# Two-layer encoder trunk on one core: sums of the modulation vectors moved to VectorE in the first phase, and to other places later on

## The chip, the core and the metric

The kernel runs on one core of a Trainium2 chip. The metric is the device time of one execution in microseconds (us), median over the runs. The engines of the core are TensorE (PE in the views, with PEld for its weight loads), VectorE (DVE), ScalarE (ACT), GpSimd (POOL) and SyncE (SP), which here only issues transfers. Each engine works through its own instructions in the order in which they were laid down. A scheduler of the framework lays that order down when the kernel is built, so it is not simply the order of the program text.

## The reference

For 256 tokens of width 2048 the trunk computes two layers and a final norm. Layer 0 is RWKV-7 time mixing and a squared-ReLU MLP of width 8192; layer 1 is attention in chunks of 64 tokens over a shared key and value, and another MLP. Each sub-layer is normed and modulated by vectors that come from the condition c (one vector of 2048):

```
for layer in range(DEPTH):
    mod = c @ w_ada[layer] + b_ada[layer]
    sh1, sc1, gt1, sh2, sc2, gt2 = jnp.split(mod, 6, axis=-1)
    if layer == N_A_LAYERS:
        sh_kv, sc_kv = jnp.split(c @ w_ada_kv + b_ada_kv, 2, axis=-1)
        ...
    h = modulate(rms_norm(x, g_mix[layer]), sh1, sc1)
    ...
    x = x + gt1[:, None, :] * y
    h = modulate(rms_norm(x, g_mlp[layer]), sh2, sc2)
    x = x + gt2[:, None, :] * sq_relu_mlp(h, w_up[layer], w_down[layer])
return rms_norm(x, g_final)
```

So there are 14 modulation vectors of 2048 numbers, each a product of c with a 2048 x 2048 matrix in float32 (16 MB to be read for each). This case is about where in the program, and on which engine, those products are formed.

## The kernel before

**Large products.** Every matrix product is split for precision. A tile of weights `raw` (128 x 1024, 512 KB) is loaded by SP, ScalarE casts it into `wH` (L367), and VectorE subtracts to get the rest `wL` (L370). PE then multiplies: a 512-column product with `wH` (L401) and a 256-column product with `wL` (L402) per tile of 128 inputs (`proj2`), or three products of 258 columns (L390 to L392, `proj`). There are three buffers each of `wH` and `wL`, and six of `raw`. SP issues all weight loads in one queue, in order, and an issue that waits for a free buffer holds those behind it.

**The first two modulation vectors** (scale and shift of layer 0, `ada_blocks`) are needed before anything else. They are made in eight blocks of 256 outputs. A block loads two parts of four tiles `rawa` (512 KB each, four buffers). Each tile holds four input tiles of 128 x 256. PE multiplies the four with a column of c repeated 32 times (`crep`) and puts them into four groups of 32 columns of the array (L666), so that the four run beside each other. ScalarE copies the sums to `adat` (L672), PE folds the four groups (L677), and VectorE adds the bias (`mod`, L683) and forms the gain (L685). The first block stands at the start of the program; the others are spread among the value projection, the LoRA products (`l`, from `mix` tiles that VectorE makes, L707) and the second half of that projection (`t`, added into `v` on VectorE, L734). This is phase 1; it ends near 217 us.

**The other twelve vectors** are summed up on VectorE. A step (`ada_step`) takes one tile of 128 x 1024 of a modulation matrix (`raw`, or `rada` where a pool of its own was opened by `ada_room`) and adds its product with one number of c per partition to `acc` (L441 for the first tile of 16, L443 for the others). There are 384 steps. After 16 of them PE folds `acc` (`ada_sum`, L465). The steps are spread over the program as follows:

- In the time mixing there are 19 periods of 16 slots. Six slots of each period take a step, from the third period (p = 2) on: 102 steps.
- In the first `out_proj` (the product with `w_o`, tiles n = 0 to 15), a pool of five `rada` buffers is open, tiles 8 and 9 take a step, and the last six tiles drain the queue.
- In the MLPs, `ada_tick` takes three steps in two tiles. Where a vector is needed and not complete, `ada_need` takes the missing steps at once; behind the up products of the first 16 tiles it asks for vector (0, 5), which is complete at step 128.
- At the end of the first MLP the last seven tiles drain the queue.

**Norms.** The sum of squares `ss` of the new x is complete when the last tile of `out_proj` or of an MLP is (VectorE adds the last part, L507). PE then sums it over the partitions (L512, in `rstd`), and VectorE and ScalarE make the factor `rstd` (`rv` L514, L519 to L521). To keep PE fed meanwhile, the next stage starts with eight output tiles on inputs that are not normed yet (the constant `RAW`), and multiplies by `rstd` afterwards (`late_norm`, L553 and L554). The product for `rstd` stands behind the first eight of the 16 input tiles of the first of them (constant `HK`).

In the period loop the slots that take a step are set by hand:

```
if slot in self.ADA_SLOTS and p >= 2:
    self.ada()
```

Of the kernel before, what the change touches and what calls it, by code (L numbers as in the profile page):

```python
# [12 lines left out]
F32 = mybir.dt.float32  # L13
# [304 lines left out]
class Body:  # L318
# [243 lines left out]
    def run(self):  # L562
# [22 lines left out]
        with ExitStack() as st:  # L585
# [6 lines left out]
            self.ada_need((0, 2), (0, 4), (0, 3))  # L592
            with self.ada_room(5):
                nxt = self.out_proj(self.pp, "w_o", self.y_hl, (0, 2), "g_mlp0", (0, 4), (0, 3), self.o_ps)
            sp.close()
# [24 lines left out]
    def layer_a(self, st, sp):  # L620
# [6 lines left out]
        with ExitStack() as s1:  # L627
# [22 lines left out]
            def ada_blocks():  # L650

                lo = 0
                for w_ in blocks:
                    W, ks = w_ * P, 8 // w_
                    ps = self.psm().rearrange("p (i n) -> p i n", i=2)
                    for part in (1, 0):
                        w, _ = self.ada_src(0, part)
                        w = w[:, lo * P:lo * P + W].rearrange("(a i p) n -> a p i n", p=P, i=ks)
                        for a in range(KT // ks):
                            raw = pb.tile([P, HK * P], F32, tag="rawa", bufs=4, name="rawa")  # L660
                            raw = raw.rearrange("p (i n) -> p i n", i=ks)
                            nc.sync.dma_start(out=raw, in_=w[a])
                            for i in range(ks):
                                kt = ks * a + i
                                g = 32 * (kt % 4)
                                nc.tensor.matmul(ps[g:g + 32, part, :W], crep[:, kt, :], raw[:, i, :],  # L666
                                                 start=(part == 1 and kt < 4), stop=(part == 0 and kt >= KT - 4),
                                                 tile_position=(0, g))
                            if part or a < KT // ks - 1:
                                yield  # L670
# [119 lines left out]
        with ExitStack() as s1:  # L790
# [50 lines left out]
            for p in range(NPAIR + 3):  # L841
# [11 lines left out]
                for slot in range(16):  # L853
# [9 lines left out]
                    self.fin(2)  # L863
                    if slot in self.ADA_SLOTS and p >= 2:
                        self.ada()
# [4 lines left out]
    def out_proj(self, pp, wname, hl, gate, g, sc, sh, begun=()):  # L870
# [5 lines left out]
        for n0 in range(0, KT, 2):  # L876
# [14 lines left out]
            for n, ps in zip((n0, n0 + 1), sums):  # L891
# [7 lines left out]
                self.ss_add(x, n, nc.vector if n == KT - 1 else None)  # L899
                if n < KT - 6 and (n >= 8 or not begun):  # L900
                    self.ada()
                elif n >= KT - 6:
                    self.ada_drain(1)
# [7 lines left out]
    def mlp(self, st, pp, layer, scaled, gain, shift, g=None, sc=None, sh=None):  # L911
# [8 lines left out]
        def up(q, f):  # L920
# [5 lines left out]
            if q == 0 and f < RAW:  # L926
                ins = self.proj(ps[:, :TE], w, lambda kt: scaled[:, kt], (0, HK))
                if rstd is None:
                    with tc.issue_after(ins):
                        rstd = self.rstd()  # L930
                self.proj(ps[:, :TE], w, lambda kt: scaled[:, kt], (HK, KT))
                self.late_norm(t, ps, rstd, ALU.max, 0.0)
            else:
                ps = ps.rearrange("p (i t) -> p i t", i=2)
                self.proj2(ps, w, lambda kt: hl[:, kt, :, 0:T])
                self.sum2(t, ps)
                nc.scalar.activation(t, t, AF.Relu)  # L937
# [7 lines left out]
        for q in range(NQ):  # L945
# [13 lines left out]
            for n in range(KT):  # L959
# [7 lines left out]
                if q == NQ - 1:  # L967
# [5 lines left out]
                    if g is None:  # L973
                        nc.scalar.activation(x, x, AF.Copy, scale=self.vec("g_final", n))
                if q == NQ - 1 and n >= KT - 7:
                    self.ada_drain(1)
# [9 lines left out]
    def attention(self, st, pp, scaled, kv_gain, kv_shift):  # L986
# [20 lines left out]
        for j in range(RAW):  # L1007
            ps = pp.tile([P, 512], F32, tag="pj", bufs=2, name="pj")
            w = self.weight(d["w_k_shared"][j])
            ins = self.proj(ps[:, :TE], w, lambda kt: scaled[:, kt], (0, HK))  # L1010
            if rstd is None:
                with tc.issue_after(ins):
                    rstd = self.rstd()
            self.proj(ps[:, :TE], w, lambda kt: scaled[:, kt], (HK, KT))
            self.late_norm(ks[:, j, :], ps, rstd, ALU.bypass, None)
# [158 lines left out]
```

## Time and profile before

| what | value |
|---|---|
| median of three runs | 2722.8 us (2720.47 to 2723.33) |
| the profiled execution | 2719.8 us, of which the span of the records is 2718.0 us |
| mean granted TensorE clock | 0.994 |
| DVE, ACT, POOL busy | 2072.1 us (76%), 1348.1 us (50%), 227.4 us (8%) |
| moved by DMA | 662.65 MB, 244 GB/s in the mean |

The stages in the trace of before are: phase 1 to about 217 us, the time mixing and its drain to about 750 us (the first row of L894 starts at 750.6), the first `out_proj` from there to 817 us (`rv` at 817.5), the first MLP to 1556 us, the attention with its two projections after that, and the second MLP to the end.

A row of the timeline gives the start, the duration, the engine, the line, what it writes and reads, and in brackets how long the engine was idle before it and what ended that. A row of the waits gives the engine, line and releaser, then the us in total, the number of times and the longest. A row of the windows gives the busy time of each engine in a stretch, then the mean granted TensorE clock (PEclk), the DMA share and the GB/s.

### The profile page before, as it was taken

The numbers are of one execution on the slowest core, as the hardware profiler recorded it, in microseconds if no ns is written. First come the engines' busy times: TensorE is split into PE (matmuls) and PEld (weight loads), VectorE is DVE, ScalarE is ACT, GpSimd is POOL, SyncE is SP. The second block draws the span as 40 slices with busy tenths as digits, with TensorE's granted clock in tenths as the row PEclk, the third lists the DMA queues.
The fourth block names the chain that finished last, engine by engine and source line by source line (L and its number), as shares of the span: only waits on it lengthen the run. The fifth ranks groups of instructions, "written<-read, shape, count | busy, mean of one in ns | idle before, by whom it ended". The sixth has DMA issues, their size and how long they took to land.

```text
span 2718.0 us, 58600 instructions
## 1 busy us (share of the span) xinstructions
PE 2649.5 (97%) x23786; PEld 2237.3 (82%) x23786; DVE 2072.1 (76%) x3045; ACT 1348.1 (50%) x2432; POOL 227.4 (8%) x368
## 2 busy tenths in 40 slices
PE   6999999999999999999999999999999999999997
PEld 3678777777889888888888898877898888888886
DVE  4568878877798988888888996898988555555555
ACT  2346544545356445445355454465565364453554
POOL 0002223323110000000000100000100000000002
PEclk9999999999999999999999999999999999999999
DMA  9876556554687988888888877887857555555553
GB/s 312 277 276 204 181 164 200 186 180 153 194 292 250 354 313 314 326 300 318 320 325 324 280 265 237 315 295 230 290 184 266 190 189 186 186 187 187 188 190 125
DMA packets 217390, 662.65 MB, mean 244 GB/s; under 512 B 21408, under 2 KB 68896, under 8 KB 217120
## 3 DMA queue, kind: packets, MB, share of 16 engines
q1 hardware_dynamic: 215056, 656.36, 70.4%
q8 instruction: 187, 3.06, 0.5%
q10 hardware_dynamic: 2064, 2.54, 0.3%
q14 instruction: 83, 0.68, 0.1%
HBM read 656.72 MB, written 2.10 MB: 242 GB/s over the span
## 4 chain that ended last, share of the span: by engine, by line
PE 88%; DVE 4%; DMA 3%; issue 3%; ACT 1%; POOL 0%; DVEq 0%; SPq 0%; ACTq 0%; POOLq 0%
PE pj L401 44%; PE pj L402 22%; PE iv L106 2%; DVE wL L370 2%; PE pj L391 1%; PE pj L392 1%; PE pj L390 1%; PE gr L100 1%; DVE acc L443 1%; PE m L666 1%; PE ms L100 1%; PE o L390 1%; DMA rada<-w_ada 1%; PE chn L270 1%; PE ms L110 1%
## 5 line engine op out<-in xcount | busy, mean ns | idle before, releaser
L370 DVE TENSOR_TENSOR wL<-raw,wH 128x1024 fp32r<-128x1024 f32 x772 | 942.3, 1222 | 370.1 <-ACT wH L367 366.3
L401 PE MATMUL pj<-aHL,wH 128*128 128x512 f32 x3328 | 1217.6, 406 | 2.0 <-DVE x L894 1.1
L367 ACT CAST wH<-raw 128x1024 fp32r<-128x1024 f32 x772 | 805.6, 1045 | 801.6 <-PE pj L401 585.9
L402 PE MATMUL pj<-aHL,wL 128*128 128x256 f32 x3328 | 939.9, 282 | 4.3 <-DVE wL L370 4.3
L401 PEld LDWEIGHTS pj<-aHL,wH 128*128 128x128 f32 x3328 | 629.4, 189 | 155.7 <-issue 11.8
L401 PE MATMUL pj<-hHL,wH 128*128 128x512 f32 x2048 | 722.6, 398 | 2.8 <-ACT wH L367 2.8
L402 PEld LDWEIGHTS pj<-aHL,wL 128*128 128x128 f32 x3328 | 629.9, 189 | 9.0 <-DVE wL L370 5.7
L402 PE MATMUL pj<-hHL,wL 128*128 128x256 f32 x2048 | 574.8, 281 | 0.8 <-DVE wL L370 0.8
L401 PEld LDWEIGHTS pj<-hHL,wH 128*128 128x128 f32 x2048 | 385.6, 188 | 95.7 <-ACT wH L367 3.2
L402 PEld LDWEIGHTS pj<-hHL,wL 128*128 128x128 f32 x2048 | 387.9, 189 | 1.2 <-DVE wL L370 1.1
L443 DVE SCALAR_TENSOR_TENSOR acc<-rada,ct,acc 128x1024 f32<-128x1024 f32 x265 | 339.5, 1281 | 7.6 <-DMA rada<-w_ada 6.9
L507 POOL TENSOR_TENSOR ss<-ss,sq 128x256 f32<-128x256 f32 x56 | 53.5, 956 | 1594.2 <-ACT sq L506 1593.9
L965 DVE SCALAR_TENSOR_TENSOR x<-pj,mod,x 128x256 f32<-128x256 f32 x256 | 123.3, 482 | 55.4 <-PE pj L402 52.0
L443 DVE SCALAR_TENSOR_TENSOR acc<-raw,ct,acc 128x1024 f32<-128x1024 f32 x95 | 124.4, 1310 | 4.6 <-DMA raw<-w_ada 4.5
L391 PE MATMUL pj<-aHL,wH 128*128 128x258 f32 x384 | 109.6, 286 | 0.0
L390 PE MATMUL pj<-aHL,wH 128*128 128x258 f32 x384 | 109.6, 285 | 0.0
L392 PE MATMUL pj<-aHL,wL 128*128 128x258 f32 x384 | 108.7, 283 | 0.8 <-DVE wL L370 0.8
L937 ACT ACTIVATE t<-t 128x256 f32<-128x256 f32 x112 | 46.8, 418 | 111.4 <-DVE t L909 111.3
L392 PEld LDWEIGHTS pj<-aHL,wL 128*128 128x128 f32 x384 | 74.0, 193 | 1.1 <-DVE wL L370 1.1
L391 PEld LDWEIGHTS pj<-aHL,wH 128*128 128x128 f32 x384 | 73.4, 191 | 0.1
L390 PEld LDWEIGHTS pj<-aHL,wH 128*128 128x128 f32 x384 | 73.0, 190 | 0.2
L666 PE MATMUL m<-rawa,crep 128*32 128x256 f32 x512 | 46.2, 438 | 16.7 <-DMA rawa<-w_ada 16.2
(240 smaller groups left out, 2807.8 us busy)
## 6 DMA issues: line engine op xcount, KB each, us to landing
raw<-w_up SPq DMA_DIRECT2D x256, 512.0 KB, 4.5
raw<-w_down SPq DMA_DIRECT2D x256, 512.0 KB, 4.6
rada<-w_ada SPq DMA_DIRECT2D x218, 512.0 KB, 5.7
raw<-w_ada SPq DMA_DIRECT2D x102, 512.0 KB, 4.1
rawa<-w_ada SPq DMA_DIRECT2D x64, 512.0 KB, 6.7
rada<-w_ada_kv SPq DMA_DIRECT2D x64, 512.0 KB, 6.8
raw<-w_k SPq DMA_DIRECT2D x32, 512.0 KB, 4.9
raw<-w_r SPq DMA_DIRECT2D x32, 512.0 KB, 4.4
```

The lines of the kernel that those rows point to most:

```text
L100: self.b.nc.tensor.matmul(o(c)[K], lhsT(c)[K], rhs(c)[K], start=True, stop=True)
L106: self.b.nc.tensor.matmul(o[QS[K], c, :], lhsT[QS[R], c, :], rhs[QS[R], c, :], start=True, stop=True, tile_position=(H * R, H * K))
L367: nc.scalar.copy(Hf, raw)
L370: eng.tensor_tensor(out=Lf, in0=raw, in1=Hf, op=ALU.subtract)
L390: nc.tensor.matmul(ps, H[:, i, :], a(kt)[:, 0, :], start=(first and kt == 0), stop=False)
L391: nc.tensor.matmul(ps, H[:, i, :], a(kt)[:, 1, :], start=False, stop=False)
L392: ins = nc.tensor.matmul(ps, L[:, i, :], a(kt)[:, 0, :], start=False, stop=(last and kt == KT - 1))
L401: nc.tensor.matmul(ps, H[:, i, :], a(kt), start=(kt == 0), stop=False)
L402: ins = nc.tensor.matmul(ps[:, 0, :], L[:, i, :], a(kt)[:, 0, :], start=False, stop=(kt == KT - 1))
L443: nc.vector.scalar_tensor_tensor(out=self.acc, in0=raw, scalar=ck, in1=self.acc, op0=ALU.mult, op1=ALU.add)
L666: nc.tensor.matmul(ps[g:g + 32, part, :W], crep[:, kt, :], raw[:, i, :], start=(part == 1 and kt < 4), stop=(part == 0 and kt >= KT - 4), ...
L965: nc.vector.scalar_tensor_tensor(out=x, in0=ps[:, i, :], scalar=self.mods[(layer, 5)][:, n:n + 1], in1=x, op0=ALU.mult, op1=ALU.add)
```

## The change

It has four parts.

1. In `ada_blocks` the last of the four `rawa` tiles of each part is no longer multiplied on PE. VectorE multiplies its four input tiles by their numbers of c and adds them up in `acca` (one tensor_scalar and three scalar_tensor_tensor of 128 x 256), and PE adds `acca` with one product with ones (32 columns). `rawa` gets six buffers instead of four.
2. The time mixing takes steps from its first period on (12 more steps: 114). The first `out_proj` has no pool and takes none.
3. The product for `rstd` stands behind 12 input tiles instead of eight at the start of the MLPs and of the attention.
4. At the end of the first MLP the last nine tiles drain the queue, instead of the last seven.

```
@@ run
             self.ada_need((0, 2), (0, 4), (0, 3))
-            with self.ada_room(5):
-                nxt = self.out_proj(self.pp, "w_o", self.y_hl, (0, 2), "g_mlp0", (0, 4), (0, 3), self.o_ps)
+            nxt = self.out_proj(self.pp, "w_o", self.y_hl, (0, 2), "g_mlp0", (0, 4), (0, 3), self.o_ps)
@@ ada_blocks
                         for a in range(KT // ks):
-                            raw = pb.tile([P, HK * P], F32, tag="rawa", bufs=4, name="rawa")
+                            raw = pb.tile([P, HK * P], F32, tag="rawa", bufs=6, name="rawa")
                             raw = raw.rearrange("p (i n) -> p i n", i=ks)
                             nc.sync.dma_start(out=raw, in_=w[a])
-                            for i in range(ks):
-                                kt = ks * a + i
-                                g = 32 * (kt % 4)
-                                nc.tensor.matmul(ps[g:g + 32, part, :W], crep[:, kt, :], raw[:, i, :],
-                                                 start=(part == 1 and kt < 4), stop=(part == 0 and kt >= KT - 4),
-                                                 tile_position=(0, g))
+                            if a == KT // ks - 1:
+                                acc = pb.tile([P, W], F32, tag="acca", bufs=2, name="acca")
+                                for i in range(ks):
+                                    ck = self.ct[:, ks * a + i:ks * a + i + 1]
+                                    if i == 0:
+                                        nc.vector.tensor_scalar(out=acc, in0=raw[:, i, :], scalar1=ck, scalar2=0.0,
+                                                                op0=ALU.mult, op1=ALU.add)
+                                    else:
+                                        nc.vector.scalar_tensor_tensor(out=acc, in0=raw[:, i, :], scalar=ck, in1=acc,
+                                                                       op0=ALU.mult, op1=ALU.add)
+                                nc.tensor.matmul(ps[0:32, part, :W], self.cst("ones")[:, 0:32], acc,
+                                                 start=False, stop=(part == 0), tile_position=(0, 0))
+                            else:
+                                for i in range(ks):
+                                    kt = ks * a + i
+                                    g = 32 * (kt % 4)
+                                    nc.tensor.matmul(ps[g:g + 32, part, :W], crep[:, kt, :], raw[:, i, :],
+                                                     start=(part == 1 and kt < 4),
+                                                     stop=(part == 0 and g > 0 and kt >= KT - ks - 4),
+                                                     tile_position=(0, g))
@@ layer_a, the period loop
-                    if slot in self.ADA_SLOTS and p >= 2:
+                    if slot in self.ADA_SLOTS:
                         self.ada()
@@ out_proj
-                if n < KT - 6 and (n >= 8 or not begun):
+                if n < KT - 6 and not begun:
                     self.ada()
                 elif n >= KT - 6:
                     self.ada_drain(1)
@@ mlp
-                ins = self.proj(ps[:, :TE], w, lambda kt: scaled[:, kt], (0, HK))
+                ins = self.proj(ps[:, :TE], w, lambda kt: scaled[:, kt], (0, 12))
...
-                self.proj(ps[:, :TE], w, lambda kt: scaled[:, kt], (HK, KT))
+                self.proj(ps[:, :TE], w, lambda kt: scaled[:, kt], (12, KT))
...
-                if q == NQ - 1 and n >= KT - 7:
+                if q == NQ - 1 and n >= KT - 9:
                     self.ada_drain(1)
@@ attention
-            ins = self.proj(ps[:, :TE], w, lambda kt: scaled[:, kt], (0, HK))
+            ins = self.proj(ps[:, :TE], w, lambda kt: scaled[:, kt], (0, 12))
...
-            self.proj(ps[:, :TE], w, lambda kt: scaled[:, kt], (HK, KT))
+            self.proj(ps[:, :TE], w, lambda kt: scaled[:, kt], (12, KT))
```

In the changed kernel the lines behind `ada_blocks` carry other numbers: the packed products are L679, the product with ones L673, the fold L691, the add into `v` L748, the sums of `out_proj` into x L908.

Where the steps stand in the order of the instructions is seen at three places, all on VectorE.

**The end of phase 1.** `v` is the sum of the value projection, `aHL<-h` the splitting of the inputs of r, `acc` the steps, `wL` the weight halves, `k` the first output of the time mixing. Before:

```order
L734 TENSOR_TENSOR v<-v,t 128x512
L370 TENSOR_TENSOR wL<-raw,wH 128x1024
L734 TENSOR_TENSOR v<-v,t 128x512
L370 TENSOR_TENSOR wL<-raw,wH 128x1024
L560 TENSOR_TENSOR aHL<-h,aHL 128x256 x16
L370 TENSOR_TENSOR wL<-raw,wH 128x1024
```

Now:

```order
L748 TENSOR_TENSOR v<-v,t 128x512
L441 TENSOR_SCALAR acc<-raw,ct 128x1024
L370 TENSOR_TENSOR wL<-raw,wH 128x1024
L748 TENSOR_TENSOR v<-v,t 128x512
L443 SCALAR_TENSOR_TENSOR acc<-raw,ct,acc 128x1024
L370 TENSOR_TENSOR wL<-raw,wH 128x1024
L748 TENSOR_TENSOR v<-v,t 128x512
L443 SCALAR_TENSOR_TENSOR acc<-raw,ct,acc 128x1024
L560 TENSOR_TENSOR aHL<-h,aHL 128x256 x16
L370 TENSOR_TENSOR wL<-raw,wH 128x1024
```

Three steps stand ahead of the splits, and one `wL` more than before stands behind them.

**The tiles 8 and 9 of the first `out_proj`.** `x` is the new residual stream, `aHL<-x` the inputs of the MLP. Before:

```order
L443 SCALAR_TENSOR_TENSOR acc<-rada,ct,acc 128x1024
L370 TENSOR_TENSOR wL<-raw,wH 128x1024
L894 SCALAR_TENSOR_TENSOR x<-pj,mod_2_72,x 128x256
L443 SCALAR_TENSOR_TENSOR acc<-rada,ct,acc 128x1024
L894 SCALAR_TENSOR_TENSOR x<-pj,mod_2_72,x 128x256
L443 SCALAR_TENSOR_TENSOR acc<-rada,ct,acc 128x1024
L539 SCALAR_TENSOR_TENSOR aHL<-x,gain_g_mlp_11163,aHL 128x256
L443 SCALAR_TENSOR_TENSOR acc<-rada,ct,acc 128x1024
L370 TENSOR_TENSOR wL<-raw,wH 128x1024
```

Now:

```order
L908 SCALAR_TENSOR_TENSOR x<-pj,mod_2_72,x 128x256 x2
L370 TENSOR_TENSOR wL<-raw,wH 128x1024
L539 SCALAR_TENSOR_TENSOR aHL<-x,gain_g_mlp_11263,aHL 128x256
L370 TENSOR_TENSOR wL<-raw,wH 128x1024
L908 SCALAR_TENSOR_TENSOR x<-pj,mod_2_72,x 128x256 x2
```

The steps are gone from here. The scheduler has drawn steps of the MLP's ticks forward into the later tiles: 11 of them stand between tile 10 and the `rv` of the norm, where there were four.

**The start of the first MLP.** `rv`, `ru` and `rstd` are the norm's steps. Before:

```order
L507 TENSOR_TENSOR ss<-ss,sq 128x256
L514 TENSOR_SCALAR rv<-m 128x256
L370 TENSOR_TENSOR wL<-raw,wH 128x1024
L519 SCALAR_TENSOR_TENSOR ru<-rstd 128x256
L520 TENSOR_TENSOR ru<-ru,rv 128x256
L521 SCALAR_TENSOR_TENSOR rstd<-ru,rstd 128x256
```

Now:

```order
L514 TENSOR_SCALAR rv<-m 128x256
L443 SCALAR_TENSOR_TENSOR acc<-rada,ct,acc 128x1024
L519 SCALAR_TENSOR_TENSOR ru<-rstd 128x256
L443 SCALAR_TENSOR_TENSOR acc<-rada,ct,acc 128x1024
L520 TENSOR_TENSOR ru<-ru,rv 128x256
L370 TENSOR_TENSOR wL<-raw,wH 128x1024
L521 SCALAR_TENSOR_TENSOR rstd<-ru,rstd 128x256
```

Two steps now stand inside the norm.

On SP, the eight loads of `w_down` that follow the up products now stand in a row ahead of the next `rada`; before, one or two `rada` stood ahead of each. Vector (0, 5) is complete before the last up tile, so `ada_need` takes no step there. At the end of the first MLP the steps that stood in its last tiles and inside the norm (nine of them) now come later, in the attention's first stages.

## The prediction

> **What bounds the kernel now.** I read the page's busy table first, then the waits of PE by stage, then the timeline around the long waits, then the windows for the granted clock.
>
> ```profile
> span 2718.0 us, 58600 instructions
> PE 2649.5 (97%) x23786; PEld 2237.3 (82%) x23786; DVE 2072.1 (76%) x3045; ACT 1348.1 (50%) x2432; POOL 227.4 (8%) x368
> ```
>
> PE is idle for 2718.0 − 2649.5 = 68.5 us of the span. The change takes hardly any product away, so that is what can be gained. The waits of PE to 205 us, then one row from 1000 to 1700 us:
>
> ```profile
> PE m L666 <- DMA rawa<-w_ada: 16.2, 8, 9.5
> PE l L754 <- DVE mix L707: 6.8, 5, 2.6
> PE t L726 <- DVE v L734: 3.6, 3, 1.6
> ...
> PE pj L392 <- DVE wL L370: 0.8, 1, 0.8
> ```
>
> The first waits lie in phase 1 and are mostly the first loads. Behind phase 1 three places carry the loss. PE's rows at them, and what the clock did there:
>
> ```profile
> 778.49 0.58 PE L402 MATMUL pj<-aHL,wL 128*128 128x256 f32 x1 [2.11 <-DVE wL L370]
> 921.17 0.49 PE L401 MATMUL pj<-hHL,wH 128*128 128x512 f32 x1 [2.85 <-ACT wH L367]
> 922.43 0.58 PE L402 MATMUL pj<-hHL,wL 128*128 128x256 f32 x1 [0.77 <-DVE wL L370]
> 1559.16 0.67 PE L512 MATMUL m<-ss,csts 128*128 128x256 f32 x2 [2.70 <-DVE ss L507]
> ```
>
> ```profile
> 778.00:782.00 4.00, 3.51 (x12) 3.09 (x13) 4.00 (x6) 0.81 (x2) 0.66 (x1) 0.57 0.79 266
> 921.00:925.00 4.00, 3.06 (x9) 2.46 (x10) 3.85 (x4) 2.21 (x3) 0.00 (x0) 0.57 1.02 407
> 925.00:929.00 4.00, 4.00 (x15) 3.37 (x15) 1.86 (x3) 1.04 (x1) 0.00 (x0) 0.57 1.02 411
> 1560.00:1564.00 4.00, 4.00 (x23) 4.00 (x23) 3.90 (x6) 0.84 (x2) 0.00 (x0) 0.59 0.91 282
> ```
>
> After each wait the granted clock falls to 0.57 to 0.59 for 4 us, after the double one for 8 us. A window of 4 us at 0.57 loses 0.43 x 4 = 1.7 us, which comes on top of the wait. The Trainium skill ("TensorE: Matmul & The Clock Gate", Part 1) says that the clock is halved after an idle window of about 3.4 us. By that rule none of these waits is long enough, and a removed wait would be worth its own length alone. This trace differs: 2.11 us brought 0.57.
>
> **What removes the three.** At 775 us, VectorE has steps between the weight halves:
>
> ```profile
> 772.36 1.27 DVE L443 SCALAR_TENSOR_TENSOR acc<-rada,ct,acc 128x1024 f32<-128x1024 f32 x1
> ...
> 773.95 1.27 DVE L443 SCALAR_TENSOR_TENSOR acc<-rada,ct,acc 128x1024 f32<-128x1024 f32 x1
> ...
> 776.02 1.27 DVE L443 SCALAR_TENSOR_TENSOR acc<-rada,ct,acc 128x1024 f32<-128x1024 f32 x1
> 777.22 1.22 DVE L370 TENSOR_TENSOR wL<-raw,wH 128x1024 fp32r<-128x1024 f32 x1
> ```
>
> These steps are no longer at tiles 8 and 9, so `wL` comes over 2.11 us earlier: **−3.8** (2.11 + 1.7). At 918 us the queue of SP and ScalarE's row tell it:
>
> ```profile
> 907.43 4.63 SPq L357 DMA_DIRECT2D rada<-w_ada_kv  x3
> 912.11 0.90 SPq L357 DMA_DIRECT2D raw<-w_down  x2
> ```
>
> ```profile
> 920.08 1.04 ACT L367 CAST wH<-raw 128x1024 fp32r<-128x1024 f32 x1 [7.28 <-DMA raw<-w_down]
> ```
>
> Three `rada` issues hold SP for 4.63 us until buffers come free, and `w_down` is issued only at 912.11 and lands at 920. With eight `w_down` ahead of the next `rada` and no forced steps this goes: **−7.0** (2.85 + 0.77 + 2 x 1.7). At 1556 us the last part of `ss` is late behind steps and their loads:
>
> ```profile
> 1553.10 1.61 DVE L443 SCALAR_TENSOR_TENSOR acc<-rada,ct,acc 128x1024 f32<-128x1024 f32 x1 [1.21 <-DMA rada<-w_ada]
> ...
> 1558.60 0.42 DVE L507 TENSOR_TENSOR ss<-ss,sq 128x256 f32<-128x256 f32 x1
> ```
>
> The nine steps leave this place, and the product for `rstd` comes four input tiles later. Products of that kind follow each other in 0.12 us:
>
> ```profile
> 826.07 0.28 PE L391 MATMUL pj<-aHL,wH 128*128 128x258 f32 x1
> 826.19 0.28 PE L392 MATMUL pj<-aHL,wL 128*128 128x258 f32 x1
> ```
>
> Four input tiles take twelve of them, 1.4 us. Both together exceed 2.70: **−4.4** (2.70 + 1.7), and **−0.8** for the `pj L392` wait, the same backlog. The steps that move behind it fall into the attention's tiles. I cost them at nothing there; if VectorE has no room, they cost up to 1 us.
>
> **What is added.** *Phase 1.* 64 small VectorE operations and 16 products replace 16 groups of four packed ones.
>
> ```profile
> L707 DVE SCALAR_TENSOR_TENSOR mix<-xx,vecs,h 128x256 f32<-128x256 f32 x80 | 36.6, 508 | 5.4 <-POOL xx L702 2.9 <-PE l L758 2.1 <-PE l L754 0.4
> L683 DVE TENSOR_TENSOR mod<-m,bada 128x2 f32<-128x2 f32 x16 | 1.8, 154 | 50.7 <-PE m L677 50.7
> ```
>
> ```profile
> 110.06 0.64 PE L666 MATMUL m<-rawa,crep 128*32 128x256 f32 x8
> 110.63 0.39 PE L762 MATMUL v<-aHL,wH 128*128 128x256 f32 x1
> ...
> 119.90 1.10 PE L754 MATMUL l<-mix,lw 128*96 128x256 f32 x4 [0.63 <-DVE mix L707]
> ```
>
> The nearest VectorE form takes 0.51 us, so four take about 1.7 to 2.0 us, 64 some 30 us. VectorE waits 50.7 us for the folds, some 6 us per block, and half of the new work falls into that; the other half stands among the `mix` tiles. On PE a packed group takes 0.57 to 0.64 us and an unpacked float32 product 1.10 / 2 = 0.55 us. So a group saves between nothing and 0.2 us, where the new product follows another packed group: I take 0.1 x 16 = −1.6. The Trainium skill ("TensorEngine Tiling (Array Packing)", Key Properties) states that the tiles of an array run in parallel. By that rule four packed products cost what one costs, the −1.6 would be nothing and the sum 1.6 us higher; the rows of 0.64 and 0.55 us agree with it nearly.
>
> The fold now waits for load, four sums, product and copy in turn; PE has four short products between the new product and the fold to cover the copy. Bounds per block are 0 and 1 us; I take 0.3 for seven blocks, +2.1. Phase 1 behind its start: **+0.5** (−3 to +6). The six buffers let loads start earlier, which matters only if the loads are late, and after 31 us PE waits for none.
>
> *The start.* PE waits there for the loads (16.2 us). Behind the eighth, four sums and one product now stand where a packed group stood: four times 0.4 to 0.5 us, **+1.5** (1 to 2).
>
> *The start of the time mixing.*
>
> ```profile
> 214.40 1.23 DVE L370 TENSOR_TENSOR wL<-raw,wH 128x1024 fp32r<-128x1024 f32 x1 [0.28 <-ACT wH L367]
> 216.28 0.69 DVE L734 TENSOR_TENSOR v<-v,t 128x512 f32<-128x512 f32 x1 [0.65 <-PE t L728]
> 217.24 1.23 DVE L370 TENSOR_TENSOR wL<-raw,wH 128x1024 fp32r<-128x1024 f32 x1 [0.27 <-ACT wH L367]
> 218.38 5.45 DVE L560 TENSOR_TENSOR aHL<-h,aHL 128x256 fp32r<-128x256 f32 x16
> ...
> 217.11 0.47 PE L401 MATMUL pj<-aHL,wH 128*128 128x512 f32 x1 [0.87 <-DVE v L734]
> ...
> 235.87 0.76 DVE L441 TENSOR_SCALAR acc<-raw,ct 128x1024 f32<-128x1024 f32 x1
> ```
>
> ```profile
> 236.00:260.00 24.00, 23.84 (x376) 18.44 (x375) 23.27 (x45) 14.23 (x35) 8.61 (x13) 1.00 0.65 208
> ```
>
> PE already waits for the last `v`. Two steps ahead of it (0.76 + 1.27) meet idle time of 0.65 + 0.28 us, so it is about 1 us later. The third step and a `wL` behind the splits delay r's products by about another 1.1 us. From 236 us on VectorE has 0.7 us free in 24, so the other steps of the first two periods (some nine, 1.27 us each) delay what the pairs need of VectorE. The later cover is three buffers of halves and the other pairs' products. Bounds for that rest are 0 and 8 us; I take 2.4, nearer to nothing, since PE's small products of one pair leave the large ones to run. Together **+4.5** (2 to 10).
>
> *The start of the first MLP.*
>
> ```profile
> 817.49 0.42 DVE L514 TENSOR_SCALAR rv<-m 128x256 f32<-128x256 f32 x1 [0.79 <-PE m L512]
> ...
> 824.12 1.22 DVE L370 TENSOR_TENSOR wL<-raw,wH 128x1024 fp32r<-128x1024 f32 x1
> ```
>
> ```profile
> 820.00:840.00 20.00, 19.90 (x40) 1.00 0.81 280
> ```
>
> That `wL` ends at 825.34, 0.85 us ahead of its product at 826.19 (quoted above). Now the norm starts 1.4 us later, two steps stand in it (2 x 1.2) and half a `late_norm` more stands ahead of that `wL` (0.5): 4.3 − 0.85 = **+3.5**. VectorE is full there (19.90 of 20), so nothing absorbs it; the bounds are 0, if the steps find VectorE early, and 8, if most of the seven further steps of the tiles before (seven times 1.27) add to it. *The second MLP* starts in the same way without the steps: 1.4 − 0.85 = **+0.5**.
>
> **The sum.** −3.8 − 7.0 − 5.2 + 0.5 + 1.5 + 4.5 + 3.5 + 0.5 = −5.5 on the profiled 2719.8, so 2714.3. The median lies 3.0 above that execution: **2717**.
>
> **Rivals.** (1) *VectorE at its limit gives everything back.* In the first periods (236 to 260 us) and from tile 10 to the first MLP it is full, and each step there becomes PE time as soon as its slack is used, 0.85 us in the second place. With both terms at their far end, 10 and 8: −5.5 + 5.5 + 4.5 = +4.5, with two halved clocks (1.7 each) +8, 2731. For it speak the busy rows; against it, that VectorE drops as many steps elsewhere. (2) *Phase 1's longer chain to the fold.* 1 us and more at each block and no saving on PE: +0.5 becomes +7, the time 2724. For it: PE's waits for `mix` and `v` are already 10.4 us; against: VectorE's 50.7 idle us. (3) *The delays are hidden.* The two starts cost 2 and 1, phase 1 gains 3: −5.5 − 2.5 − 2.5 − 3.5 = −14, 2709. (4) *The halved clock does not go with the waits*: the 6.8 us of it (four times 1.7) come back at other places, and the sum is +1.3, 2724. The rows have it directly behind each of the three waits, so I give it little. The rule of the Trainium skill named above would come to this. (5) *The scheduler puts the steps back in front of the same halves*: the order shows it does not at 775 us, but the eleven steps after tile 10 are that case in part, priced under (1).
>
> **Chances.** Forecast 0.47, rival 1 0.25, rival 2 0.09, rival 3 0.16, rival 4 0.03. The range: the forecast's own is 2710 to 2724; 2704 to 2735 takes in most of the rivals. A measurement of this kernel can tell about 0.2%, 5.4 us, from no change. Faster by more (under 2717.4): 0.28 of the forecast, all of rival 3, 0.44. Slower by more (over 2728.2): 0.21 of rival 1, 0.04 of rival 2, 0.02 of the forecast, 0.27. Within: 0.29.
>
> **What would show it.** The three waits (775, 918, 1556 us) and the halved clock behind them gone; new waits of PE on VectorE near 217 to 260 us and on `wL` near 826 us; in phase 1 short waits of the fold for `adat` and no long one of L673 for `acca`. The forecast is wrong if a wait of over 2 us with a halved clock stands at one of the three places, if phase 1 ends more than 7 us later, or if the time mixing, from its first product to the drain, takes over 10 us longer.

## The result, and the profile after

| | before | changed |
|---|---|---|
| median | 2723.87 us (22 runs, 2719.3 to 2729.7) | 2719.27 us (22 runs, 2714.6 to 2731.6) |
| ratio to before | | 0.9987, 95% interval 0.9979 to 0.9995 |
| profiled execution | 2719.8 us, span 2718.0 | 2718.15 us, span 2716.3 |

The change makes the kernel 0.13% faster, some 3.5 us; the forecast was −5.5 us. The page of the changed kernel:

```profile
span 2716.3 us, 58473 instructions
PE 2646.6 (97%) x23690; PEld 2237.0 (82%) x23690; DVE 2098.3 (77%) x3109; ACT 1347.4 (50%) x2432; POOL 235.0 (9%) x368
```

VectorE is busy 26 us longer (64 small sums), PE has 96 records less. PE's waits by stage in the changed kernel, from 26 to 212 us, from 205 to 760 us and from 740 to 1700 us (line, releaser, us in total, times, longest; the rows left out are marked):

```profile
PE t L740 <- DVE v L748: 2.7, 3, 1.2
...
PE m L673 <- DVE acca L671: 2.1, 3, 1.8
PE l L768 <- DVE mix L721: 2.0, 3, 1.0
...
PE gr L100 <- DVE bh L169: 3.2, 1, 3.2
...
PE iv L106 <- DVE tt L229: 2.8, 3, 1.6
PE pj L402 <- DVE e L812: 1.7, 1, 1.7
PE pj L401 <- DVE v L748: 1.4, 1, 1.4
...
PE m L512 <- DVE ss L507: 2.8, 1, 2.8
PE o L392 <- DVE wL L370: 2.7, 2, 2.0
PE pj L392 <- DVE wL L370: 1.5, 1, 1.5
```

The waits at 775, 918 and 1556 us are gone; between 1000 and 1700 us PE waits for nothing at all. In their place stand waits of the time mixing's start and of the first MLP's. In phase 1 the waits for `mix` fell from 6.8 to 2.0 us. The longest rows at the new places, and the clock there:

```profile
240.38 0.90 PE L100 MATMUL gr<-kr,bh 64*64 64x128 f32 x5 [3.22 <-DVE bh L169]
763.73 0.38 PE L392 MATMUL o<-aHL,wL 128*128 128x256 f32 x1 [1.96 <-DVE wL L370]
825.49 0.70 PE L512 MATMUL m<-ss,csts 128*128 128x256 f32 x2 [2.75 <-DVE ss L507]
```

```profile
236.00:260.00 24.00, 18.17 (x252) 13.73 (x253) 20.60 (x36) 10.43 (x28) 8.95 (x11) 0.86 0.73 247
824.00:828.00 4.00, 2.51 (x13) 2.46 (x14) 3.40 (x5) 0.94 (x2) 0.00 (x0) 0.81 1.02 383
828.00:832.00 4.00, 4.00 (x29) 4.00 (x28) 3.73 (x6) 1.85 (x4) 0.00 (x0) 0.77 0.87 291
```

The clock of 0.86 over 24 us costs 0.14 x 24 = 3.4 us, the other two windows (0.19 + 0.23) x 4 = 1.7 us. Behind the wait at 763 us the clock is 0.72 from 764 to 770 us, another 1.7 us. To see where time went stage by stage, the starts of PE rows that both traces have are compared:

| place | before | changed | difference |
|---|---|---|---|
| fold of the first block | 25.57 | 27.45 | +1.9 |
| first product of the time mixing | 217.11 | 210.42 | −6.7 |
| third pair's `gr` products | 296.86 | 302.47 | +5.6 |
| first `o` product | 671.34 | 677.84 | +6.5 |
| product for `rstd`, first MLP | 816.76 | 825.49 | +8.7 |
| first down product | 906.22 | 916.62 | +10.4 |
| second group of down products | 1097.13 | 1099.31 | +2.2 |
| product for `rstd`, second MLP | 1984.86 | 1980.99 | −3.9 |
| first down product, second MLP | 2074.31 | 2069.05 | −5.3 |
| end of the span | 2718.0 | 2716.3 | −1.7 |

Two cautions belong to this table. The trace of before lies 4.1 us below the median of its kernel and that of the changed kernel 1.1 us below, so the last row is some 3 us short of the difference of the medians (4.6 us). And by part 3 the products for `rstd` stand four input tiles (1.4 us) later in the order, which moves these two rows without any loss.

### The profile page after: what moved, and what is told of

Same layout as the page of the kernel before. It is cut to its first block, busy times and chain, and to the rows that moved or that the text cites. A ratio compares the mean times of both kernels' runs of the same rounds, so it can differ in the third digit from the quotient of the medians.

```text
span 2716.3 us, 58473 instructions
## 1 busy us (share of the span) xinstructions
PE 2646.6 (97%) x23690; PEld 2237.0 (82%) x23690; DVE 2098.3 (77%) x3109; ACT 1347.4 (50%) x2432; POOL 235.0 (9%) x368
## 4 chain that ended last, share of the span: by engine, by line
PE 86%; DVE 4%; DMA 2%; issue 2%; ACT 1%; POOL 0%; DVEq 0%; SPq 0%; ACTq 0%; POOLq 0%
PE pj L401 45%; PE pj L402 22%; PE iv L106 2%; PE pj L391 2%; PE pj L392 2%; PE pj L390 2%; PE gr L100 1%; DVE wL L370 1%; DVE acc L443 1%; PE ms L100 1%; PE o L390 1%; PE ms L110 1%; PE chn L270 1%; DMA rada<-w_ada 1%; PE chn L277 1%
## 5 line engine op out<-in xcount | busy, mean ns | idle before, releaser
L443 DVE SCALAR_TENSOR_TENSOR acc<-rada,ct,acc 128x1024 f32<-128x1024 f32 x254 | 324.9, 1279 | 7.4 <-DMA rada<-w_ada 7.0
L443 DVE SCALAR_TENSOR_TENSOR acc<-raw,ct,acc 128x1024 f32<-128x1024 f32 x106 | 139.4, 1315 | 6.3 <-DMA raw<-w_ada 6.2
L951 ACT ACTIVATE t<-t 128x256 f32<-128x256 f32 x112 | 46.8, 418 | 128.2 <-DVE t L923 128.2
L953 ACT ACTIVATE t<-t 128x256 f32<-128x256 f32 x128 | 53.4, 417 | 3.5
```

The source lines that it names most:

```text
L443: nc.vector.scalar_tensor_tensor(out=self.acc, in0=raw, scalar=ck, in1=self.acc, op0=ALU.mult, op1=ALU.add)
```

## The experiments

The ratios are to the kernel before on the same chip, with their 95% intervals. Differences in us at a place are of the profiled executions.

**Part 1 alone, and its two halves.** Three runs on the kernel before: the whole of part 1; the sums with four buffers; the six buffers without the sums.

```
-  raw = pb.tile([P, HK * P], F32, tag="rawa", bufs=4, name="rawa")
+  raw = pb.tile([P, HK * P], F32, tag="rawa", bufs=6, name="rawa")
```

The first run has this line and the diff of `ada_blocks` shown with the change, the second that diff without this line, the third this line alone.

> Only part 1 of the change (VectorE sums the fourth tile, six buffers) on the kernel before. Theory A, the parts are independent: the first product of the time mixing starts at about 210 us as in the changed kernel (217.1 before), the time mixing then runs as before, and the time is 6 to 7 us lower, ratio about 0.9975. Theory B, the time mixing cannot use an earlier start, since its first loads and VectorE are late anyway: the start is at 210 us, but the third pair's products stand at 264 us as before, ratio 0.999 to 1.001.

> Part 1 with four buffers as before, so only the sums move to VectorE. If the sums make phase 1 shorter (fewer packed products on PE and another order at the block borders): first product of the time mixing at 210 to 212 us, ratio as for part 1 whole, within 0.001. If the two more buffers do it: 216 us or later, since a buffer is now held until VectorE has summed it, and ratio 1.000 or above.

> Only the six buffers, all products on PE as before. If the sums make phase 1 shorter: first product of the time mixing at 216 to 218 us, ratio 0.9995 to 1.0005. If the buffers do it: 210 to 212 us, ratio about 0.998.

| run | first product of the time mixing | third pair | ratio |
|---|---|---|---|
| part 1 | −6.8 | −7.4 | 0.9986 (0.9976 to 0.9996) |
| sums, four buffers | −5.4 | −6.0 | 0.9980 (0.9970 to 0.9989) |
| six buffers alone | +3.2 | +3.3 | 1.0002 (0.9993 to 1.0011) |

The sums make phase 1 shorter, the buffers do not. Over all fourteen traces of this case the time mixing starts at 208.8 to 212.6 us in the eleven with the sums, and at 217.1 to 221.0 us in the three without. The +3.2 of the third run arise between 47 and 80 us, where its clock is 0.79 (0.95 before), and show in another run whose phase 1 is that of before (part 2 alone, +3.9), so they are scatter. The time mixing keeps the earlier start to the third pair (theory A); at the first `o` product 4.9 us of it are left, and the ratio lies between the two that were expected. Waits of PE to the time mixing's first product, with part 1, then with the buffers alone:

```profile
PE t L740 <- DVE v L748: 2.7, 3, 1.2
...
PE l L768 <- DVE mix L721: 1.9, 3, 1.0
```

```profile
PE l L754 <- DVE mix L707: 6.0, 4, 2.5
PE t L726 <- DVE v L734: 3.6, 3, 1.6
```

What shrinks is PE's wait at each block border. Before, PE at the fifth border:

```profile
118.05 0.38 PE L726 MATMUL t<-aHL,wH 128*128 128x256 f32 x1 [0.81 <-ACT v L732]
...
119.90 0.46 PE L754 MATMUL l<-mix,lw 128*96 128x256 f32 x1 [0.63 <-DVE mix L707]
```

The changed kernel there:

```profile
114.37 0.64 PE L679 MATMUL m<-rawa,crep 128*32 128x256 f32 x8
...
116.29 0.67 PE L768 MATMUL l<-mix,lw 128*96 128x256 f32 x2
```

Between the fold and the first `l` product PE now has a packed group and 24 `t` products to do, where it had 20, while VectorE makes the `mix` tiles, and it does not wait for them. That this order is what shortens the waits is read from it, at this border, and was not tried by itself. From the second fold to the first product of the time mixing, the windows of PE add up as follows, before (with one of its windows, clock in the third column from the end) and in the change (sum of the windows, and of PE's busy time in them):

```profile
66.86:91.73 24.87, 22.22 (x196) 0.93 0.82 276
...
sum 169.82, PE 156.40; mean PE 22.34
```

```profile
sum 160.62, PE 151.87; mean PE 21.70
```

So of 9.2 us PE's idle time gives 4.7 (13.4 to 8.7) and its busy time 4.5. Part of the busy time is clock: the window shown loses 0.07 x 24.87 = 1.7 us in before, and the change loses none in any of the seven. By that estimate some 2.8 us are work, 0.23 us for each of the 12 groups in this stretch. Over the fourteen traces the idle time here is 8.0 to 10.3 us with the sums and 12.8 to 14.1 us without.

**Part 2 alone.** Steps from the first period on, no pool and no steps in `out_proj`, on the kernel before.

```
-  if slot in self.ADA_SLOTS and p >= 2:
+  if slot in self.ADA_SLOTS:
...
-  with self.ada_room(5):
-      nxt = self.out_proj(...)
+  nxt = self.out_proj(...)
...
-  if n < KT - 6 and (n >= 8 or not begun):
+  if n < KT - 6 and not begun:
```

> Only part 2 of the change (steps from the first period on, none in the first out_proj). Theory A, the steps themselves delay the first periods through VectorE: the time mixing is 12 us longer as in the changed kernel, the stalls at 775 and 918 us go, the norm's product waits over 2 us for the last part of the squares, and the time is 4 to 9 us higher, ratio 1.0015 to 1.0035. Theory B, the loss in the changed kernel's first periods comes from its earlier start, whose loads are then late: the time mixing is only about 5 us longer, ratio 0.998 to 1.001.

Measured: 1.0038 (1.0025 to 1.0051), 10 us slower. From the first product of the time mixing to the third pair it loses 13.4 us (+3.9 to +17.3), about as the changed kernel does (12.3); at the first MLP PE waits 5.2 us for `ss`, at the attention 4.3 us. Theory A: the loss is the steps' own, and not due to the earlier start.

**The sums or the loads.** The changed kernel with 11 of the 12 sums of the first two periods cut down.

```
+  n = 8 if (key, half) == ((0, 2), 0) and kt < 12 else HK * P
-  nc.vector.scalar_tensor_tensor(out=self.acc, in0=raw, scalar=ck, in1=self.acc, ...)
+  nc.vector.scalar_tensor_tensor(out=self.acc[:, :n], in0=raw[:, :n], scalar=ck, in1=self.acc[:, :n], ...)
```

> The changed kernel with the sums of steps 2 to 12 cut to 8 of their 1024 columns; the rest of these sums is left out, their loads stay. If the sums on VectorE make the start of the time mixing late: the wait for bh goes (3.2 us), and the third pair's products stand at 291 to 294 us instead of 302. If the loads in front of the weights make it late: they stay at 300 us or later, and new waits for wH on its loads show.

Measured: 0.9965 (0.9953 to 0.9977). The stretch from the first product to the third pair loses 4.0 us instead of 12.3. The wait for `bh` falls from 3.2 to 0.6 us. The longest wait that is left stands just ahead of that stretch (PE's waits from 205 to 300 us, then VectorE's rows):

```profile
PE pj L401 <- ACT aHL L561: 3.1, 1, 3.1
...
PE gr L100 <- DVE bh L169: 0.6, 1, 0.6
```

```profile
211.66 0.23 DVE L444 SCALAR_TENSOR_TENSOR acc<-raw,ct,acc 128x8 f32<-128x8 f32 x1 [2.51 <-DMA raw<-w_ada]
211.80 0.68 DVE L750 TENSOR_TENSOR v<-v,t 128x512 f32<-128x512 f32 x1
```

A step stands ahead of the last `v`, and VectorE waits 2.5 us for its load; PE's first product comes at 212.63 us, 2.2 us later than in the changed kernel. So the sums are some 8 of the 12 us of the stretch, and a late load in front of work that PE waits for shows once the sums no longer cover it. Of the 4.0 us that remain PE's idle time gives 1.6. The rest is busy time, among it the fold of a vector that before comes later; it was not taken apart. The third pair stands at 296.4 us, between the two ranges that were expected.

**The place of the product for rstd (part 3 undone).** The same edit stands at the start of the attention.

```
-  ins = self.proj(ps[:, :TE], w, lambda kt: scaled[:, kt], (0, 12))
+  ins = self.proj(ps[:, :TE], w, lambda kt: scaled[:, kt], (0, HK))
...
-  self.proj(ps[:, :TE], w, lambda kt: scaled[:, kt], (12, KT))
+  self.proj(ps[:, :TE], w, lambda kt: scaled[:, kt], (HK, KT))
```

> The changed kernel with the product for rstd behind eight input tiles again. My sum had 1.4 us per place. If that is right where PE waits for ss at the first MLP (2.75 us now): 4.1 to 4.6 us there, with the further steps of the norm earlier by the same, so that the MLP's down products stand 0 to 2 us later; at the attention a wait of 1 to 3 us comes back; ratio to before 0.9985 to 1.001. If the place does not matter: all within 1 us of the changed kernel, ratio 0.998 to 0.9995.

Measured: 0.9987 (0.9977 to 0.9998), the time of the changed kernel. PE waits 5.6 us for `ss` at the first MLP instead of 2.75 (4.1 to 4.6 was expected), but the wait of 1.5 us for `wL` behind it is gone, and the first down product, counted from the first `o` product, is 2.5 us later. At the attention no wait over 0.3 us comes back, against the expectation. So the four input tiles move a wait more than they remove one; an effect on the whole time is not shown.

**The drain at the end of the first MLP (part 4 undone).**

```
-  if q == NQ - 1 and n >= KT - 9:
+  if q == NQ - 1 and n >= KT - 7:
```

> The changed kernel with the last seven tiles of the first MLP draining the queue, as before, instead of nine. If the steps in the last tiles and inside the norm made the wait at 1556 us: PE waits for ss at the attention again, 1 to 2.7 us, with or without a halved clock (1.7 us more), ratio 0.999 to 1.0005. If the later product for rstd alone covers it: no wait there, and the time of the changed kernel within 0.001.

Measured: 1.0023 (1.0010 to 1.0037): two tiles less of draining cost more than the whole change gains, and more than either expectation had. VectorE's rows around the norm of the attention, and the windows (clock in the third column from the end):

```profile
1561.68 1.29 DVE L443 SCALAR_TENSOR_TENSOR acc<-rada,ct,acc 128x1024 f32<-128x1024 f32 x1 [1.33 <-DMA rada<-w_ada]
...
1564.01 0.42 DVE L514 TENSOR_SCALAR rv<-m 128x256 f32<-128x256 f32 x1
1566.67 1.29 DVE L443 SCALAR_TENSOR_TENSOR acc<-rada,ct,acc 128x1024 f32<-128x1024 f32 x1 [2.23 <-DMA rada<-w_ada]
1567.87 0.42 DVE L519 SCALAR_TENSOR_TENSOR ru<-rstd 128x256 f32<-128x256 f32 x1
```

```profile
1560.00:1570.00 10.00, 9.51 (x55) 9.36 (x56) 6.43 (x10) 3.03 (x5) 0.00 (x0) 0.67 0.80 269
1570.00:1580.00 10.00, 7.54 (x51) 7.37 (x50) 8.74 (x19) 4.47 (x8) 0.18 (x2) 0.83 0.89 294
```

Between `rv` and `ru` VectorE waits 2.23 us for the load of a step that stands in front of them. PE waits 2.5 us for `ss` and 2.5 us for `ks`, and 0.33 x 10 + 0.17 x 10 = 5.0 us of clock are lost. Where the steps stand in the order, counted per weight half, explains it. They come in runs of 16 (one half of a vector), and in this order a run was drawn forward up to its end where it had begun before the norm. With nine tiles the steps stop at 288 = 18 x 16, and none stands near the norm; with seven, 10 further ones stand ahead of `rv` and two more inside the norm. That the runs of 16 are the cause is read from the order and was not tried by itself.

**Steps in later periods.** The changed kernel with steps from the third period on and seven slots in each (119 steps), then with six slots (102).

```
-  if slot in self.ADA_SLOTS:
+  if slot in self.ADA_SLOTS and p >= 2:
```

and, with seven, also

```
-  ADA_SLOTS = (1, 3, 6, 9, 11, 14)
+  ADA_SLOTS = (1, 3, 5, 7, 9, 11, 14)
```

> The change with steps from the third period on, but seven slots in each period instead of six (119 steps before the first out_proj instead of 114, none in it, as in the change). Theory A, the 12 us that the time mixing lost are due to the steps in its first two periods, where VectorE is full, and its later periods have room: the third pair's products stand at about 290 us (302 in the changed kernel, 297 before), the waits at 775 and 918 us stay away, ratio to before 0.993 to 0.996. Theory B, VectorE has no room in the later periods either, and 17 steps of 1.28 us show there in full or in half: the time mixing is 10 to 20 us longer behind 300 us, ratio 0.998 to 1.002.

> The changed kernel with steps from the third period on and six slots, so 102 steps before the first out_proj, and none in it. The start of the time mixing should be as before the change (third pair's products at 289 to 291 us). 26 steps are then missing for vector (0, 5) at the first out_proj. If the loads of missing steps, put ahead of w_down, made the wait at 918 us: a wait for wH or wL of 2 us or more near 905 to 915 us and a halved clock come back, and the down products start as before but end 5 to 9 us later against the run with seven slots. If only the steps in out_proj made both waits: none there, and a ratio like that of seven slots, 0.992 to 0.995.

Measured with seven: 0.9932 (0.9916 to 0.9947), median 2704.28 us. The third pair stands at −2.7 us against before (294.2 us; 290 was expected), and the first `o` product at −1.5 us. One step more than before stands ahead of the third pair, and the stretch to it is 3.2 us longer, with a wait of 1.9 us and a halved clock. The 14 more steps from there to the first `o` product cost 1.1 us, not 10. PE's waits from 740 to 1700 us:

```profile
PE m L512 <- DVE ss L507: 7.3, 2, 5.0
PE o L392 <- DVE wL L370: 1.2, 2, 0.8
PE pj L392 <- DVE wL L370: 0.4, 1, 0.4
```

With six: 0.9996 (0.9985 to 1.0006). The time mixing, from its first product to the first `o` product, is 0.5 us longer than before (4.4 us with seven slots), but 26 steps are missing at the first MLP, and the way from the product for `rstd` to the second group of down products is 18 us longer than with seven slots (+7.7 against −10.7 to the kernel before). SP's queue and PE's waits (740 to 1000 us):

```profile
916.23 7.71 SPq L357 DMA_DIRECT2D rada<-w_ada_kv  x5
923.99 0.42 SPq L357 DMA_DIRECT2D raw<-w_down  x1
925.93 6.83 SPq L357 DMA_DIRECT2D rada<-w_ada_kv  x4
932.81 0.42 SPq L357 DMA_DIRECT2D raw<-w_down  x1
```

```profile
PE pj L401 <- ACT wH L367: 5.6, 2, 3.3
PE m L512 <- DVE ss L507: 4.1, 1, 4.1
PE pj L402 <- DVE wL L370: 2.7, 4, 1.5
...
```

That is the mechanism of the wait at 918 us, larger: the loads of steps hold SP for 7.7 and 6.8 us in front of two loads of `w_down`.

**The steps around the norms.** Three runs on the one with seven slots: 13 tiles draining; an eighth slot in the last eight periods as well (127 steps); the same in the last seven (126).

```
-  if q == NQ - 1 and n >= KT - 9:
+  if q == NQ - 1 and n >= KT - 13:
```

and, with 127 steps (`p >= 12` with 126), also

```
-  if slot in self.ADA_SLOTS and p >= 2:
+  if p >= 2 and slot in self.ADA_SLOTS or p >= 11 and slot == 13:
```

> The run with seven slots, with the last 13 tiles of the first MLP draining instead of nine, and nothing else. By the order the first MLP's tail then holds no step behind its third tile, as in the changed kernel, and 16 steps move into the attention's first tiles. If those steps made the 5.0 us wait for ss: it goes, and the attention's end stands 5 to 8 us earlier than with seven slots, ratio 0.9905 to 0.9925. If the 16 steps cost the attention as much: the attention's end at the same time as with seven slots, ratio 0.993.

> The run with seven slots, with an eighth slot in the last eight periods (127 steps before the first out_proj) and the last 13 tiles of the first MLP draining instead of nine. If steps in the tail of out_proj and in the last tiles of the MLP make the waits for ss at both norms (2.4 and 5.0 us with seven slots, the latter with 2 to 3 us of halved clock): both under 1 us, ratio 0.990 to 0.993. If VectorE's own work of the norm makes them: they stay over 2 us, ratio 0.993 to 0.995. If the eighth slot is too much for the late periods: the first product of out_proj over 3 us later than with seven slots.

> The run with 127 steps before the first out_proj, with 126 (the eighth slot one period later). By the order this has no step inside the norm before the second MLP, where the run with 127 had five, and the first norms stay as they are there. If those five made the loss at the second MLP (waits of 1.6, 3.0 and 1.1 us and 6.6 us between the norm and the down products): it goes, the second MLP's down products stand 19 to 21 us ahead of the kernel before, ratio 0.991 to 0.993. If the loss is due to the other order of the attention: the waits stay, ratio 0.994 to 0.996.

| run | wait for `ss`, first MLP | attention | second MLP | ratio |
|---|---|---|---|---|
| seven slots | 2.4 | 5.0 | none | 0.9932 (0.9916 to 0.9947) |
| 13 tiles draining | 2.9 | none | none | 0.9921 (0.9906 to 0.9936) |
| 127 steps | none | none | 1.6, and 3.0 for `wH` | 0.9952 (0.9937 to 0.9967) |
| 126 steps | none | none | none | 0.9931 (0.9917 to 0.9944) |

Each wait went or came as the order had it. With 127 steps VectorE has this in front of the second MLP:

```profile
1965.07 0.41 DVE L507 TENSOR_TENSOR ss<-ss,sq 128x256 f32<-128x256 f32 x1
1965.41 2.59 DVE L443 SCALAR_TENSOR_TENSOR acc<-rada,ct,acc 128x1024 f32<-128x1024 f32 x2
...
1969.05 0.41 DVE L514 TENSOR_SCALAR rv<-m 128x256 f32<-128x256 f32 x1
1969.39 1.27 DVE L443 SCALAR_TENSOR_TENSOR acc<-rada,ct,acc 128x1024 f32<-128x1024 f32 x1
```

Five sums stand between the last part of `ss` and `rstd`. One step less before the first `out_proj` takes them out, two stages later, and the second MLP's first down product stands 6.4 us earlier. The whole times of the runs with 13 tiles, 126 steps and seven slots are not told apart by their intervals: what the first norms gain is partly lost elsewhere (with 126 steps PE waits 3.0 us for `vt` in the attention). With 13 tiles the gain is seen in the stretch that it was expected in: from the last group of down products to the end of the attention it is 5.6 us shorter than with seven slots. But the execution profiled was already 6.6 us later there, in an order that is the same up to that point, so the attention's end itself is not earlier. The lowest median, 2699.98 us with 13 tiles, beats both kernels of this case.

## Why the prediction was right, and where its terms were not

The forecast of 2717 us and a small gain held (2719.27, ratio 0.9987), but in part by luck: two errors cancel, phase 1 (9.1 us better than forecast) and the time mixing (8.7 us worse). The gain is also smaller than the likeliest outcome. The prediction gave 0.44 to a gain of more than 0.2%, and 0.29 to a change within 0.2%, which is what came. Term by term, in us, from the table of places:

| term | forecast | measured |
|---|---|---|
| the start | +1.5 | +1.9 |
| phase 1 behind it | +0.5 (−3 to +6) | −8.6 |
| start of the time mixing | +4.5 (2 to 10) | +12.3 to the third pair, +13.2 to the first `o` product |
| 775 us, and start of the first MLP | −3.8 + 3.5 | +3.9 |
| 918 us | −7.0 | −8.2 |
| 1556 us, and start of the second MLP | −5.2 + 0.5 | −7.5 |
| from there to the end | none | +3.6 |

- **The three waits** went as forecast, each with its halved clock. The measured terms also contain waits that the forecast did not count: 1.4 us at 1062 us, and 1.0 us at 1722 us with 1.7 us of halved clock behind it. Rival 4 had 6.8 us of halved clock coming back at other places. That much did come back, 3.4 us between 236 and 260 us and 1.7 us behind each of the waits at 763 and 825 us, but behind new waits and not by itself.
- **Phase 1** is the step that failed. The forecast took 1.6 us of saved PE work (0.1 us for each of 16 groups) and added 2.1 us for the longer chain to the fold, with PE's order at the block borders as given. What the runs showed in place of that 2.1: PE's idle time fell by 4.7 us, where the scheduler laid products behind the fold in which PE had waited, and 1.7 us of halved clock went with it. The saved work is some 2.8 us over 12 groups. The rule of the Trainium skill ("TensorEngine Tiling (Array Packing)", Key Properties) would have had no saving. This trace shows some 0.23 us less for each group taken out, an estimate from the windows, though not whether that is the group itself or the change of array mode around it.
- **The start of the time mixing** was mis-sized, above its upper bound. By the sign that the prediction itself named, a time mixing over 10 us longer, this part of it was wrong. The mechanism was the one named (VectorE full in the first periods, `bh` late, `v` late). From the first product to the third pair PE is idle for 7.4 us more than before (8.3 against 0.9) and the clock costs 3.4 us, together 10.8 of the 12.3 us. The forecast had left the clock out of this term, and put the rest "nearer to nothing", since other products would run meanwhile. None does where `gr` stands: PE idles there for 3.22 us. Part 2 alone, 1.0038, shows what rival 1 would have made of the time without the gain in phase 1.
- **The start of the first MLP** lies near the upper bound (+7.7 beside −3.8 for the removed wait). Its new costs are 2.0 at 763 us, 2.4 more for `ss`, 1.5 for `wL` and 3.4 of clock (1.7 each behind the first two); they come to 9.3, and a wait of 0.9 us at 719 us that went is part of the difference. The 0.85 us of slack and the two steps in the norm were the right mechanism. The wait at 763 us was not named, and that the steps drawn into `out_proj` make `ss` itself late only as the far end.
- **Parts 3 and 4** were costed together at 1556 us. The runs separate them: without part 4 the change is slower than before (1.0023), and part 3 alone moves nothing that the whole time shows. With part 1 at 0.9986 and part 2 at 1.0038 the parts multiply to 0.9986 x 1.0038 x 0.9987 / 1.0023 = 0.9988, about the whole change.
- The last 3.6 us stay open: no wait of PE in the second MLP behind its start differs. At least 1.6 us of them look like scatter, since behind the start of the last down group the trace with six buffers alone is longer than that of before by as much, with the same program.

## What to carry to other kernels

Filler work that a scheduler spreads over an in-order engine shows in the time where that engine has no slack, above all between a last sum and the norm that waits for it; look for it in the order there, and let a run of it end before such a place. Move filler out of the first periods of a pipeline, where VectorE was full here, into its steady part: 12 steps cost 12 us at the start, while 17 later ones made the time mixing about 4 us longer (4.4 against 0.5 us with seven and six slots). A forecast of a moved part has to look at the order of all engines around it, since the time may come from work that the scheduler shifts into an old wait.

## What the hardware showed

The clock's halving is not a function of the wait's length alone. Up to the first MLP, the runs with seven slots and with 13 tiles draining have the same order on PE, VectorE and SP. PE waits for `ss` there 2.36 us in the one and 2.88 us in the other; with seven slots the clock is 1.00 from 812 us on, with 13 tiles it is halved behind the wait. The windows from 816 to 820 us, first with seven slots, then with 13 tiles:

```profile
816.00:820.00 4.00, 4.00 (x36) 4.00 (x35) 3.93 (x9) 2.45 (x4) 0.00 (x0) 1.00 1.02 389
```

```profile
816.00:820.00 4.00, 3.99 (x19) 3.94 (x20) 2.63 (x5) 2.21 (x4) 0.00 (x0) 0.60 0.97 329
```

The second loses 0.4 x 4 = 1.6 us more for the same program. In the trace of before, 2.11 us at 778 us brought a halved clock. The window of about 3.4 us that the Trainium skill states ("TensorE: Matmul & The Clock Gate", Part 1) is longer than all of these waits.

The clock records of the traces show what else decides. In all fourteen a halved clock lasts 3.41 us or a multiple of it (the one that runs on to the end of the records apart), and begins on a grid of 3.41 us that runs through the whole execution. What matters is how long PE idles within one stretch of this grid, so a wait that falls across two stretches counts less in each. Behind the first 50 us and ahead of the last 20 us, stretches at full clock with PE idle for over half were followed by a halved one in 39 of 40 cases, with PE idle for a third to a half in 14 of 57, and below a third in one of over 10,000. The one exception above half is the wait with seven slots: 1.87 us of idle time lie in the stretch from 809.13 us, against 2.66 us with 13 tiles and 1.90 us at 778 us in before. So where the border lies near one half is not told exactly, and it is a reading of these traces, not tried by itself. A wait of 2 to 3 us thus carries 0 or 1.7 us more, and two profiles of one program can differ by that at each such place.
